# Begun blocks, sides, gate products, rotation and the first 1/rms of a two-sequence encoder layer, in another order

## The chip, the cores and the metric

One core of a Trainium2 chip runs the whole program in one launch. The metric is the device time of a launch in microseconds, of which the median over runs is taken. Two runs of one kernel that differ by less than about 0.2% are not told apart.

## The reference

Two sequences of 512 tokens by 1024 channels pass one layer. All data is float32.

```
def swiglu(x, w_gate, w_up, w_down):
    return (jax.nn.silu(x @ w_gate) * (x @ w_up)) @ w_down

def encoder_layer(x, ...):
    x = x + 0.5 * swiglu(rms_norm(x, ffn1_norm), ffn1_w_gate, ffn1_w_up, ffn1_w_down)
    h = rms_norm(x, mix_norm)
    proj = h @ w_in
    aq, ak, av, mq, mk, mv, gate_pre, o_pre, g_att, g_mlstm = jnp.split(proj, split_at, axis=-1)
    aq = apply_rope(rms_norm(aq, q_norm), cos, sin)
    ak = apply_rope(rms_norm(ak, k_norm), cos, sin)
    att = gqa_block_attention(aq, ak, av)
    mem = mlstm_bidirectional(mq, mk, mv, gate_pre, mlstm_gate_bias, o_pre, mlstm_head_norm)
    merged = jax.nn.sigmoid(g_att) * (att @ w_up_att) + jax.nn.sigmoid(g_mlstm) * (mem @ w_up_mlstm)
    x = x + merged @ w_out
    x = x + 0.5 * swiglu(rms_norm(x, ffn2_norm), ffn2_w_gate, ffn2_w_up, ffn2_w_down)
    return x
```

After the layer comes a last rms_norm. The FFN's hidden width is 2816 (22 blocks of 128), attention has 8 query heads and 2 key heads of 64 channels with a rotation by position, and the matrix memory (mlstm) has 4 heads of 128 channels in two directions, with running maxima that keep its exponentials in range.

## The kernel before

**Number format and products.** Each float32 operand is split into a high and a low part in TensorE's rounded format (ACT copies the high part, VectorE subtracts to get the low one), and each product is three matmuls: high by high, high by low, low by high. A 512 by 512 by 128 product is so 4 x 3 = 12 matmuls of 128x512 (`product`, L297).

**Stages.** FFN1 up, FFN1 down, the mix of sequence 0, the mix of sequence 1 with both output projections, FFN2 up, FFN2 down, output. Each FFN's product with its weights uses Strassen's scheme with seven products where eight would stand: the left factors are sums of gate and up weight halves, the right ones (`xc`) sums of halves of the two sequences, named B11, B21, B22, T4, T1, T2_, T3.

**FFN up.** 22 blocks of hidden columns, each with seven products into three banks of PSUM: X (mm) for B11 and B21, Y (pss) for T2_, T3, T4, and Z (pst) for T1 and B22. B11 and B21 need the first sequence alone, so some blocks (`AHEAD` of them) are *begun* early, while the second sequence is still normalised: their two results are written to memory (`kept`) and read back when the block is *resumed*, with five products then. `gu_rest` is the rest of a block: u2 is v1 plus T2_ (L326); v5 is a copy of T1 by ACT (L330); the add of T3 (L334), of v1 (L336), of B22 (L339), Silu (L341) and the add of T4 (L344) follow; and two gate products end it (L345, L346, on GpSimd). `ORDER` sets the order of blocks: a resumed and a whole block in turn, seven times, then the remaining eight whole ones. Two blocks make a pair.

**Sides.** After each block's gate products, `Sides` forms the right factors for the down stage and sends them to memory (`rbuf`): `out` copies the high part on ACT (L358), subtracts on VectorE (L359) and issues two DMAs on SyncE. `even` sends B11 of the first block of a pair, `odd` the other six.

**FFN down.** 28 steps of (product, chunk of pairs); its weights are loaded, summed and split on the way (`prep`), and the results are added to accumulators.

**Mix.** Keys and values with gates first, then queries with their norm and rotation (`q_rope`), eight attention heads with other projections filled in between (`fill`), the two up projections merged with tanh gates, and the four memory heads (`mem_head`). In `mem_head` a row of gate sums is loaded from `ebuf` to all partitions, GpSimd adds the triangular mask (L1022), VectorE takes two maxima (L1023, L1024), and some dozen tiny operations make the scales. The factor 1/rms of the first sequence (`mid_stats(0)`: transposes at L188, VectorE's steps at L166 to L177, a broadcast over TensorE at L198) is computed inside the first mix.

**What sets the order.** Instructions are issued by a scheduler that follows program order with priorities: `shifted(n)` moves what is issued inside it earlier (negative n) or later (positive n). Each engine and each queue then runs its list strictly in order, and waits at the first instruction whose operands are not there. `LATER` is 100 and `SOONER` -100. Buffers come from rings: a tile's next user waits for its last reader.

## Time and profile before

| what | value |
|---|---|
| runs of the kernel | 2181.13, 2179.64, 2176.89 us; median 2179.64 |
| the profiled execution | 2180.97 us, its span 2179.2 us |
| TensorE matmuls x9544 | 2096.6 us busy (96%) |
| VectorE x2881 | 1642.4 us (75%) |
| ACT x1699 | 954.3 us (44%) |
| GpSimd x220 | 284.3 us (13%) |
| mean TensorE clock granted | 0.988 |

The stages by the trace, in us from the span's start: FFN1 up 20 to 476, FFN1 down to 688, mix of sequence 0 to 1046, mix of sequence 1 and the output projections to 1496, FFN2 up to 1946, FFN2 down to 2153, output to 2179. In rows of the trace PE is TensorE's matmuls, PEld its weight loads, DVE VectorE, POOL GpSimd and SP SyncE, whose queue issues most DMAs. A timeline row has its start, its length in us, engine, line, operation, tiles and shapes, how many instructions it merges, and in brackets the idle time before it and what ended that. A group's row ends with busy time, mean ns of one, idle time before, and its releasers.

### The profile page before, as it was taken

To read this page: it belongs to the slowest core of one execution; us is meant where nothing else is said; L and a number is where in the kernel's file an instruction comes from. 1 tells how busy PE (TensorE), PEld (TensorE's weight loads), DVE (VectorE), ACT (ScalarE), POOL (GpSimd) and SP (SyncE) were. 2 spreads that over 40 slices of the span, in tenths; PEclk is the share of its full clock that TensorE was granted. 3 is DMA by queue.
4 is the path that set the end of the run, shared out by engine and by line. 5 is a ranking of instruction groups with operands and counts; after the bars stand their busy time and mean duration, and the time that the engine had idled before them with its cause. 6 is when DMAs were issued, how large, how long until landed. Compare 5 with 4: busy or idle time off the path is not lost.

```text
span 2179.2 us, 27321 instructions
## 1 busy us (share of the span) xinstructions
PE 2096.6 (96%) x9544; PEld 1707.3 (78%) x9544; DVE 1642.4 (75%) x2881; ACT 954.3 (44%) x1699; POOL 284.3 (13%) x220
## 2 busy tenths in 40 slices
PE   8999999999999999999999999999999999999997
PEld 6877777878888777878887887877777778878886
DVE  7888877776697797785649878766877777776695
ACT  7534443443224466463436664434434344443222
POOL 0111121111002100100121001011111111110002
PEclk9999999999999999999999999999999999999999
DMA  9565654479765122332351233357455544479752
GB/s 298 163 195 183 213 168 157 145 265 382 284 220 181 40 68 57 95 104 77 115 165 39 59 92 95 114 153 224 155 176 171 177 159 159 140 273 386 270 196 106
DMA packets 312473, 366.04 MB, mean 168 GB/s; under 512 B 18352, under 2 KB 208832, under 8 KB 311312
## 3 DMA queue, kind: packets, MB, share of 16 engines
q1 hardware_dynamic: 311744, 363.04, 50.8%
q0 software_dynamic: 592, 1.27, 0.3%
q8 instruction: 75, 1.23, 0.2%
q14 instruction: 62, 0.51, 0.1%
HBM read 255.15 MB, written 109.08 MB: 167 GB/s over the span
## 4 chain that ended last, share of the span: by engine, by line
PE 41%; DVE 7%; issue 4%; ACT 2%; POOL 1%; DMA 1%; DVEq 0%; SPq 0%; ACTq 0%; POOLq 0%
PE mm L707 14%; PE pss L297 5%; PE pst L297 4%; PE mm L541 4%; PE mm L297 2%; PE pss L541 2%; PE pst L541 2%; PE mm L691 2%; PE pso L541 1%; POOL t L346 1%; PE pso L1096 1%; PE pso L936 1%; PE pss L1047 1%; PE pss L910 1%; PE pst L929 1%
## 5 line engine op out<-in xcount | busy, mean ns | idle before, releaser
L707 PE MATMUL mm<-xh,w 128*128 128x512 f32 x896 | 293.4, 397 | 0.0
L297 PE MATMUL pst<-xc,w 128*128 128x512 f32 x1056 | 263.7, 399 | 22.3 <-ACT t L330 22.3
L297 PE MATMUL mm<-xc,w 128*128 128x512 f32 x1056 | 259.6, 393 | 7.0 <-ACT f L306 4.0
L297 PE MATMUL pss<-xc,w 128*128 128x512 f32 x1056 | 256.0, 391 | 3.9 <-DVE t L326 3.9
L297 PEld LDWEIGHTS pst<-xc,w 128*128 128x128 f32 x1056 | 202.6, 193 | 69.9 <-ACT t L330 27.4
L297 PEld LDWEIGHTS mm<-xc,w 128*128 128x128 f32 x1056 | 196.5, 188 | 54.5 <-ACT f L306 7.9
L297 PEld LDWEIGHTS pss<-xc,w 128*128 128x128 f32 x1056 | 197.0, 188 | 48.4 <-DVE t L326 7.7
L707 PEld LDWEIGHTS mm<-xh,w 128*128 128x128 f32 x896 | 167.4, 189 | 32.1
L541 PE MATMUL mm<-rt,w 128*128 128x512 f32 (+1 forms) x819 | 186.0, 383 | 0.2 <-DMA rt<-rbuf 0.2
L221 ACT ACTIVATE w<-wr 128x1024 fp32r<-128x1024 f32 (+1 forms) x112 | 114.7, 1029 | 153.5 <-issue 72.2
L707 PE MATMUL mm<-xl,w 128*128 128x512 f32 x448 | 176.9, 395 | 0.0
L541 PEld LDWEIGHTS mm<-rt,w 128*128 128x128 f32 x819 | 150.2, 188 | 30.4 <-DMA rt<-rbuf 0.6
L346 POOL TENSOR_TENSOR t<-t,t 128x512 f32<-128x512 f32 x44 | 73.1, 1661 | 715.1 <-ACT t L341 547.3
L256 DVE TENSOR_TENSOR w<-t,w 128x512 fp32r<-128x512 f32 x176 | 137.1, 793 | 38.3 <-ACT w L255 36.5
L255 ACT ACTIVATE w<-t 128x512 fp32r<-128x512 f32 x176 | 107.4, 627 | 128.9 <-DVE t L281 42.7
L222 DVE TENSOR_TENSOR w<-wr,w 128x1024 fp32r<-128x1024 f32 (+1 forms) x112 | 137.0, 1224 | 35.1 <-ACT w L221 34.6
L297 PE MATMUL pss<-xc,f 128*128 128x512 f32 x528 | 128.6, 392 | 0.6 <-DVE t L334 0.6
L297 PEld LDWEIGHTS pss<-xc,f 128*128 128x128 f32 x528 | 98.1, 188 | 24.5 <-DVE t L334 4.6
L609 ACT ACTIVATE w<-wr 128x512 fp32r<-128x512 f32 x72 | 44.4, 630 | 132.0 <-PE pso L541 63.6
L609 ACT ACTIVATE w<-t 128x512 fp32r<-128x512 f32 x82 | 51.8, 632 | 110.5 <-PE pst L541 62.3
L541 PE MATMUL pss<-rt,w 128*128 128x512 f32 x396 | 94.5, 390 | 3.4 <-DVE w L610 3.4
L707 PEld LDWEIGHTS mm<-xl,w 128*128 128x128 f32 x448 | 84.7, 189 | 16.2
(328 smaller groups left out, 3896.0 us busy)
## 6 DMA issues: line engine op xcount, KB each, us to landing
rt<-rbuf SPq DMA_DIRECT2D x154, 512.0 KB, 5.9
wr<-in_w_in_dram SPq DMA_DIRECT2D x72, 512.0 KB, 3.9
wr<-in_ffn_w_gate_dram SPq DMA_DIRECT2D x56, 512.0 KB, 4.7
rbuf<-tab SPq DMA_DIRECT2D x90, 256.0 KB, 2.7
wr<-in_ffn_w_up_dram SPq DMA_DIRECT2D x44, 512.0 KB, 4.1
rbuf<-t SPq DMA_DIRECT2D x88, 256.0 KB, 3.3
rbuf<-f SPq DMA_DIRECT2D x66, 256.0 KB, 3.0
rbuf<-R SPq DMA_DIRECT2D x64, 256.0 KB, 2.7
```

Of the source, the lines that this page charges most:

```text
L221: pin(nc.scalar.activation(hi, raw, AF.Copy))
L222: pin(lo_eng.tensor_tensor(lo, raw, f(hi), op=ALU.subtract))
L255: pin(nc.scalar.activation(t[:, 0], src, AF.Copy))
L256: pin(V_.tensor_tensor(t[:, 1], src, f(t[:, 0]), op=ALU.subtract))
L297: nc.tensor.matmul(p, a[:, k, :], xt[:, b, k, :], start=(first and k == 0 and i == 0), stop=(k == HK_ - 1 and i == 2), skip_group_check=True)
L346: G_.tensor_tensor(u2, u2, v5, op=ALU.mult)
L541: nc.tensor.matmul(p, u[:, a, d * P:(d + 1) * P], r[:, b, ts], start=(first and q == 0 and k == 0), stop=(q == len(us) - 1 and k == 2), sk ...
L609: nc.scalar.activation(hi, src, AF.Copy)
L691: nc.tensor.matmul(p[b][:, :N], a[:, k, bs], w_[:, kl, :], start=(k == 0 and i == 0), stop=(k == KD - 1 and i == 2))
L707: nc.tensor.matmul(p, a[:, k, :], b, start=(k == 0 and i == 0), stop=(k == n - 1 and i == 2))
L910: nc.tensor.matmul(p, qT[:, h, b * P:(b + 1) * P], kv[:, hk * 2 + j, :], start=(j == 0), stop=(j == 1))
L929: nc.tensor.transpose(p[:, b * P:(b + 1) * P], Ps[b][:, kb * P:(kb + 1) * P], ident)
```

## The change

Seven things are edited.

- FFN up: nine blocks are begun instead of seven (`AHEAD`), and B11 of one is issued ahead of B21 of the one before (`begin`, `begun`). The order of blocks has seven pairs of a resumed and a whole block, six whole blocks, and the last two resumed blocks at the end (`LAST`).
- The two gate products of a block are made on VectorE instead of GpSimd: 88 operations of 128x512.
- Sides: T1's side goes out in `even`, with one more tile; in `odd` only the sends of B21, T3, T2_ and T4 are issued later, not B22's and the differences.
- The rotation's product with the cosines (ten operations) is made on VectorE instead of GpSimd.
- The memory's maxima move from `mem_head` into the attention's loop (`mem_max`, one of eight rows per attention head), and the scales are computed at once for all four heads (`mem_scales`). `mem_head` loads its rows and adds the mask again (`mem_rows`), so this is done twice per row.
- The first sequence's 1/rms is computed inside the last steps of FFN1's down stage.
- Splits of weights in `load_w` are issued 60 places sooner.

TensorE's list, in FFN2's up stage, one resumed block of the kernel before: pss, pst and mm are banks of PSUM (Y, Z and X), xc the right factors, w and f the left ones. The rows are T2_, T1, a third of the next block's B11, B22, another third, T3, the last third, and the beginning of T4.

```order
L297 MATMUL pss_13531<-xc_12775,w_13363 128x512 x12
L297 MATMUL pst_13532<-xc_12776,w_13363 128x512 x12
L297 MATMUL mm_13629<-xc_12139,w_13510 128x512 x4
L297 MATMUL pst_13532<-xc_12778,w_13364 128x512 x12
L297 MATMUL mm_13629<-xc_12139,w_13510 128x512 x4
L297 MATMUL pss_13531<-xc_12777,w_13364 128x512 x12
L297 MATMUL mm_13629<-xc_12139,w_13510 128x512 x4
L297 MATMUL pss_13531<-xc_12779,f_1756_12621 128x512 x2
```

The same block of the changed kernel, in a block of other numbers:

```order
L301 MATMUL pss_13551<-xc_12713,w_13387 128x512 x12
L301 MATMUL pst_13552<-xc_12714,w_13387 128x512 x12
L301 MATMUL mm_13653<-xc_12091,w_13530 128x512
L301 MATMUL pss_13551<-xc_12715,w_13388 128x512 x12
L301 MATMUL pst_13552<-xc_12716,w_13388 128x512 x12
L301 MATMUL pss_13551<-xc_12717,f_1752_12573 128x512 x2
L301 MATMUL pss_13551<-xc_12717,f_1753_12574 128x512
```

T3 (the third pss row of twelve and more) stood behind B22 (the second pst row) with B11 pieces on either side, and stands now ahead of it, with one B11 matmul between T1 and T3; the other eleven go behind T4.

VectorE's list at the same place, up to the row that makes u2 (t<-t,pss). L359 and L365 are the low parts of sides, L256, L260, L278 to L284 and L288 belong to the weights of later blocks. The kernel before, its last twelve rows up to u2 (L326):

```order
L359 TENSOR_TENSOR t_1761_12626<-t_1761_12626,R_12633 128x512
L284 TENSOR_TENSOR t_1754_12619<-wr_13377,t_1754_12619 128x512
L359 TENSOR_TENSOR tab_12635<-t_1762_12627,tab_12635 128x512
L374 TENSOR_TENSOR t_1763_12628<-t_1763_12628,t_1765_12630 128x512
L359 TENSOR_TENSOR t_1765_12630<-t_1765_12630,R_12634 128x512
L376 TENSOR_TENSOR t_1762_12627<-t_1762_12627,t_1763_12628 128x512
L278 TENSOR_TENSOR t_1753_12618<-wr_13529 128x512
L256 TENSOR_TENSOR w_13514<-t_1755_12620,w_13514 128x512
L256 TENSOR_TENSOR w_13514<-t_1754_12619,w_13514 128x512
L359 TENSOR_TENSOR t_1763_12628<-t_1763_12628,tab_12635 128x512
L280 TENSOR_TENSOR t_1754_12619<-wr_13527,wr_13529 128x512
L326 TENSOR_TENSOR t_1765_12630<-t_1760_12625,pss_13531 128x512
```

And the changed kernel, from the add of the former block's T4 (L350) past u2 (L332):

```order
L350 TENSOR_TENSOR t_1754_12575<-t_1754_12575,pss_13405 128x512
L629 TENSOR_TENSOR f_1753_12574<-wr_13303,f_1752_12573 128x512
L351 TENSOR_TENSOR t_1758_12579<-t_1758_12579,t_1754_12575 128x512
L365 TENSOR_TENSOR R_12585<-t_1759_12580,f_1763_12584 128x512
L260 TENSOR_TENSOR w_13533<-t_1750_12571,w_13533 128x512
L379 TENSOR_TENSOR t_1759_12580<-t_1759_12580,t_1761_12582 128x512
L288 TENSOR_TENSOR t_1750_12571<-wr_13401,t_1750_12571 128x512
L332 TENSOR_TENSOR t_1761_12582<-t_1756_12577,pss_13551 128x512
L365 TENSOR_TENSOR tab_12587<-t_1758_12579,R_12586 128x512
L365 TENSOR_TENSOR t_1757_12578<-t_1757_12578,tab_12587 128x512
L260 TENSOR_TENSOR w_13534<-t_1751_12572,w_13534 128x512
L260 TENSOR_TENSOR w_13534<-t_1750_12571,w_13534 128x512
```

The row of u2 stood fourteen rows behind T4's add (L344, three rows ahead of the first row shown) and stands seven behind it now; the gate product L351 is one of the six between, and a side's difference (L379) another. On ACT four side copies (L364) stand ahead of T1's copy (L336) now, and three (L358) stood there before.

VectorE's list in the first mix where the queries are rotated, of the changed kernel (st is the tile of the memory's scales, box the ebuf row):

```order
L765 TENSOR_TENSOR t_447_5767<-t_416_5657,rs_5696 128x512
L769 TENSOR_TENSOR t_448_5769<-t_447_5767,tab_4271 128x512
L774 TENSOR_TENSOR t_449_5770<-t_447_5767,tab_4271 128x256 x2
L935 TENSOR_REDUCE st_5975<-box_5341 128x4
L776 TENSOR_TENSOR t_448_5769<-t_448_5769,t_449_5770 128x512
L882 TENSOR_TENSOR f_479_5902<-mm_5876,R_5218 128x512
```

The first reduction of `mem_max` (L935) stands ahead of the rotation's last add (L776); no such row was there before. L769 is the rotation's product, which GpSimd made.

TensorE's list around the transposes of the first 1/rms (L188). Before, among the key and value products of the first mix (L691):

```order
L691 MATMUL mm_5311<-w_5340,xh_4935 128x272 x2
L691 MATMUL mm_5311<-w_5340,xl_4936 128x272
L691 MATMUL pso_5312<-w_5340,xh_4935 128x272 x2
L691 MATMUL pso_5312<-w_5340,xl_4936 128x272
L188 MATMUL pst_5397<-ident,R_4940 128x128 x4
L691 MATMUL mm_5309<-w_5370,xh_4935 128x272 x2
L691 MATMUL mm_5309<-w_5370,xl_4936 128x272
L691 MATMUL mm_5310<-w_5370,xh_4935 128x272 x2
L691 MATMUL mm_5310<-w_5370,xl_4936 128x272
```

and now, in the last step of the down stage (L560), ahead of the mix's first products (L710):

```order
L560 MATMUL mm_5240<-rt_3747,w_3753 128x512 x6
L560 MATMUL mm_5240<-rt_3747,w_3754 128x512 x2
L188 MATMUL pst_5185<-ident,R_4956 128x128
L560 MATMUL mm_5240<-rt_3747,w_3754 128x512
L188 MATMUL pst_5185<-ident,R_4956 128x128 x3
L560 MATMUL mm_5255<-rt_3747,w_3753 128x512 x6
L560 MATMUL mm_5255<-rt_3747,w_3754 128x512 x3
L560 MATMUL pso_5270<-rt_3747,w_3753 128x512 x6
L560 MATMUL pso_5270<-rt_3747,w_3754 128x512 x3
L710 MATMUL mm_5360<-w_5351,xh_4951 128x272 x2
```

The transposes moved from the middle of the mix's first products to the last step of FFN1's down stage.

The diff:

```
@@
         pin(lo_eng.tensor_tensor(lo, raw, f(hi), op=ALU.subtract))
         return hi, lo
+    WEIGHTS = 60
     def load_w(view, lo_eng):
-        return split_w(fetch_w(view), lo_eng)
+        raw = fetch_w(view)
+        with shifted(-WEIGHTS):
+            return split_w(raw, lo_eng)
@@
-    def gu_first(W, xc, rows, between=None):
+    def gu_first_a(W, xc, v1):
         X = MM()
         product(X, W[B11], xc[B11], True)
-        v1 = rows(0)
         with shifted(SOONER):
             nc.scalar.activation(v1, X, AF.Copy)
-        if between:
-            between()
+        return X
+    def gu_first_b(X, W, xc, g0):
         product(X, W[B21], xc[B21], False)
-        g0 = rows(1)
         with shifted(SOONER):
             nc.scalar.activation(g0, X, AF.Silu)
-        return v1, g0
     def gu_rest(W, xc, got, ring, mid):
@@
             v1, g0 = got
             second()
         else:
-            v1, g0 = gu_first(W, xc, lambda i: ring("vh"[i]), second)
+            v1, g0 = ring("v"), ring("h")
+            X = gu_first_a(W, xc, v1)
+            second()
+            gu_first_b(X, W, xc, g0)
         u2 = ring("h")
         with shifted(SOONER):
             V_.tensor_tensor(u2, v1, Y, op=ALU.add)
@@
         product(Y, W[T4], xc[T4], False)
         with shifted(SOONER):
             V_.tensor_tensor(v1, v1, Y, op=ALU.add)
-        G_.tensor_tensor(g0, g0, v1, op=ALU.mult)
-        G_.tensor_tensor(u2, u2, v5, op=ALU.mult)
+        V_.tensor_tensor(g0, g0, v1, op=ALU.mult)
+        V_.tensor_tensor(u2, u2, v5, op=ALU.mult)
         return g0, u2
     class Sides:
@@
         def even(self, b11, b12):
             self.out(B11, b11)
             V_.tensor_tensor(b11, b12, b11, op=ALU.subtract)
+            self.out(T1, b11)
             self.b = b11, b12
         def odd(self, b21, b22):
             t1, b12 = self.b
-            self.out(B21, b21)
             self.out(B22, b22)
             V_.tensor_tensor(b12, b22, b12, op=ALU.subtract)
-            self.out(T3, b12, True)
             V_.tensor_tensor(b22, b22, t1, op=ALU.subtract)
-            self.out(T1, t1, True)
-            V_.tensor_tensor(b21, b21, b22, op=ALU.subtract)
-            self.out(T2_, b22, True)
-            self.out(T4, b21, True)
+            with shifted(LATER):
+                self.out(B21, b21)
+                self.out(T3, b12, True)
+                V_.tensor_tensor(b21, b21, b22, op=ALU.subtract)
+                self.out(T2_, b22, True)
+                self.out(T4, b21, True)
     LATER, SOONER = 100,-100
-    AHEAD = 7
-    ORDER = [j for p in zip(range(AHEAD), range(AHEAD, NF)) for j in p] + list(range(2 * AHEAD, NF))
+    AHEAD = 9
+    LAST = 2
+    ORDER = [j for p in zip(range(AHEAD - LAST), range(AHEAD, NF)) for j in p]
+    ORDER += list(range(2 * AHEAD - LAST, NF)) + list(range(AHEAD - LAST, AHEAD))
     class Up:
@@
         def begin(self, j, W):
             self.kept[j] = kept[j]
-            for t, d in zip(gu_first(W, self.xc, lambda _: self.ring("k")), kept[j]):
-                nc.sync.dma_start(d, t)
+            t = self.ring("k")
+            X = gu_first_a(W, self.xc, t)
+            nc.sync.dma_start(kept[j][0], t)
+            self.begun()
+            self.open = j, X, W
+        def begun(self):
+            if self.open:
+                j, X, W = self.open
+                t = self.ring("k")
+                gu_first_b(X, W, self.xc, t)
+                nc.sync.dma_start(kept[j][1], t)
+            self.open = None
         def left(self, j):
             return gu_left_a(self.fetch(j, (0,))[0])
@@
                     with shifted(LATER):
                         sides.even(*h)
                 elif i < NF - 1:
-                    with shifted(LATER):
-                        sides.odd(*h)
+                    sides.odd(*h)
@@
                              rq.unsqueeze(2).to_broadcast([P, 8, DA]), op=ALU.mult)
             o, m = T2(), T2()
             v4 = lambda x: x.rearrange("p (b h e) -> p b h e", b=nb, e=DA)
-            G_.tensor_tensor(v4(o), v4(n), cb, op=ALU.mult)
+            V_.tensor_tensor(v4(o), v4(n), cb, op=ALU.mult)
...
@@
             q_rope(b)
         go(mem_qk(0, 1), mem_qk(1, 0), mem_qk(1, 1))
+        st = spool.tile([P, 4, 2, 4, HM], F32, tag="st", bufs=1, name=nm("st"))
+        n1, bd, en, n2 = [st[:, i] for i in range(4)]
+        def mem_rows(h, d):
+            eb = T2(F32, "eb")
+            nc.sync.dma_start(eb, ebuf[d, h:h + 1, :].rearrange("a s -> (a s)").partition_broadcast(P))
+            em = T2(F32, "eb")
...
+            G_.tensor_tensor(em3, eb3, tabs[3][:, d].unsqueeze(1).to_broadcast([P, 4, P]), op=ALU.add)
+            return eb3, em3
+        def mem_max(h, d):
+            eb3, em3 = mem_rows(h, d)
+            V_.tensor_reduce(n1[:, d, :, h], em3, axis=AX.X, op=ALU.max)
+            V_.tensor_reduce(bd[:, d, :, h], eb3, axis=AX.X, op=ALU.max)
+        def mem_scales():
+            a_, x_, B_ = csv[:, 0], csv[:, 1], csv[:, 2]
+            V_.memset(en[:, :, 0], 0.0)
+            for i in range(3):
+                V_.tensor_tensor(en[:, :, i + 1], en[:, :, i], B_[:, :, i], op=ALU.add)
+                V_.tensor_tensor(en[:, :, i + 1], en[:, :, i + 1], bd[:, :, i], op=ALU.max)
...
+            nc.scalar.activation(en, en, AF.Exp, scale=-1.0)
         att = A([P, 4, 2, S], F32R, "att")
         afs = {}
@@
             nxt = scores(h + 1) if h + 1 < HA else None
             attend(h, Ps)
             Ps = nxt
+            mem_max(h // 2, h % 2)
             fill(1 if h < 4 else 2)
             if h == 2 and extra:
                 extra()
+        mem_scales()
         fill(99)
@@
         def mem_head(h):
             qk = qks[h]
...
+            ebs, ems = zip(*[mem_rows(h, d) for d in range(2)])
...
@@
         for t, kk, bank in ((x1l, k, PS), (x1u, k + HK_, PT)):
             p = turn(1, kk, [bank])
             nc.scalar.activation(t, p, AF.Copy, scale=g1[:, kk:kk + 1])
-        W.append(up.left(3 + k))
+        if k == 1:
+            up.begin(2, W[2])
+        for j in ((), (3, 4), (5, 6), (7, 8))[k]:
+            up.begin(j, up.left(j))
         put(xc[B22], k, x1u)
         right_sums(xc, k, x0l, x0u, x1l, x1u)
-        if k == 1:
-            up.begin(2, W[2])
-    for j in (3, 4, 5, 6):
-        up.begin(j, W[j])
+    up.begun()
     def late_x(j, ring):
@@
             emit_hl(xs[0][:, d, :], gm, d, *nhl[0])
         nc.sync.dma_start(xbuf[s][:, d, :], xs[s][:, d, :])
         accs[s] = sq_add(xs[s][:, d, :], accs[s], "R")
-    def mid_stats(s):
-        r[s] = stats(accs[s])
-        R[s] = bcast_cols(r[s])
+        if s == 0 and d == KD - 1:
+            mid_stats(0, 100, 140)
+    def mid_stats(s, a=0, b=0):
+        with shifted(a):
+            r[s] = stats(accs[s])
+        with shifted(b):
+            R[s] = bcast_cols(r[s])
@@
-    m0 = mix(0, *nhl[0], lambda: mid_stats(0), lambda: mid_stats(1), prep1)
+    m0 = mix(0, *nhl[0], None, lambda: mid_stats(1), prep1)
@@
             nc.sync.dma_start(t, src)
         normed(x1l, g2, R2[1], k)
         normed(x1u, g2, R2[1], k + HK_)
-        W.append(up.left(3 + k))
+        for j in ((3,), (4,), (5, 6), (7, 8))[k]:
+            up.begin(j, up.left(j))
         put(xc[B22], k, x1u)
         right_sums(xc, k, x0l, x0u, x1l, x1u)
-    for j in (3, 4, 5, 6):
-        up.begin(j, W[j])
+    up.begun()
```

More of the change, by code (lines that the diff above doesn't have):

```diff
@@ L390, in __init__ @@
             self.v = [w.rearrange("(k p) c -> p k c", p=P) for w in (wg, wu)]
-            self.kept = {}
+            self.kept, self.open = {}, None
             self.ring = Rings(s=["t2"] * 3, wd=["f2"] * 2, v=["t2"] * 3, h=["t2"] * 5, o=["f2"] * 2 + ["R"] * 2)
@@ L898, in mix @@
         go(mem_qk(0, 1), mem_qk(1, 0), mem_qk(1, 1))
+        st = spool.tile([P, 4, 2, 4, HM], F32, tag="st", bufs=1, name=nm("st"))
[4 more added lines that the diff above has]
+            em = T2(F32, "eb")
+            eb3 = eb.rearrange("p (b s) -> p b s", b=4)
+            em3 = em.rearrange("p (b s) -> p b s", b=4)
+            G_.tensor_tensor(em3, eb3, tabs[3][:, d].unsqueeze(1).to_broadcast([P, 4, P]), op=ALU.add)
[10 more added lines that the diff above has]
+                V_.tensor_tensor(en[:, :, i + 1], en[:, :, i + 1], bd[:, :, i], op=ALU.max)
+            V_.tensor_tensor(en, a_, en, op=ALU.add)
+            V_.tensor_tensor(n1, n1, x_, op=ALU.subtract)
+            V_.tensor_tensor(en, en, n1, op=ALU.max)
+            V_.scalar_tensor_tensor(bd, x_, -1.0, en, op0=ALU.mult, op1=ALU.subtract)
+            V_.tensor_tensor(n1, a_, en, op=ALU.subtract)
+            V_.tensor_tensor(n2[:, :, 2:4], n1[:, :, 2:4], B_[:, :, 1:3], op=ALU.add)
+            V_.tensor_tensor(n2[:, :, 1], n2[:, :, 3], B_[:, :, 1], op=ALU.add)
+            nc.scalar.activation(en, en, AF.Exp, scale=-1.0)
         att = A([P, 4, 2, S], F32R, "att")
```

36 lines of the change are left out of this document (4 added, 32 removed).

## The prediction

> **What bounds the kernel now.** The page comes first: engines, then the chain that ended last.
>
> ```profile
> PE 2096.6 (96%) x9544; PEld 1707.3 (78%) x9544; DVE 1642.4 (75%) x2881; ACT 954.3 (44%) x1699; POOL 284.3 (13%) x220
> PE mm L707 14%; PE pss L297 5%; PE pst L297 4%; PE mm L541 4%; PE mm L297 2%; PE pss L541 2%; PE pst L541 2%; PE mm L691 2%; PE pso L541 1%; POOL t L346 1%; PE pso L1096 1%; PE pso L936 1%; PE pss L1047 1%; PE pss L910 1%; PE pst L929 1%
> ```
>
> TensorE is the bound, and no matmul is removed, so all there is to gain is time in which it waits, or runs slowly after a wait. The odd entry is POOL t L346, a GpSimd multiply, in a chain of TensorE work. The waits view, TensorE's rows, shows who is waited for (total us, times, longest):
>
> ```profile
> PE pst L297 <- ACT t L330: 22.3, 12, 2.1
> ...
> PE mm L297 <- ACT f L306: 4.0, 5, 2.3
> PE pss L297 <- DVE t L326: 3.9, 6, 1.9
> PE pss L1047 <- DVE t L1063: 3.8, 2, 1.9
> PE pss L541 <- DVE w L610: 3.4, 2, 2.0
> ```
>
> One wait is worth more than the others together: B22 on pst for the copy at L330, twelve times, once in each resumed block that a whole pair surrounds. The timeline of one of them:
>
> ```profile
> 1576.04 1.66 POOL L345 TENSOR_TENSOR t<-t,t 128x512 f32<-128x512 f32 x1 [2.07 <-DVE t L344]
> ...
> 1577.73 0.63 ACT L358 ACTIVATE R<-t 128x512 fp32r<-128x512 f32 x1 [1.54 <-POOL t L345]
> ...
> 1579.98 0.68 DVE L374 TENSOR_TENSOR t<-t,t 128x512 f32<-128x512 f32 x1
> ...
> 1580.69 0.63 ACT L358 ACTIVATE f<-t 128x512 fp32r<-128x512 f32 x1 [2.33 <-DVE t L374]
> ...
> 1581.23 0.58 ACT L330 ACTIVATE t<-pst 128x512 f32<-128x512 f32 x1
> ...
> 1581.86 4.61 PE L297 MATMUL pst<-xc,w 128*128 128x512 f32 x12 [2.10 <-ACT t L330]
> ```
>
> T1's result is long there, but ACT runs in order: L330 stands behind side copies (L358), the last of which waits for VectorE's L374; that add, and another of the copies, wait in turn for the gate products on GpSimd. TensorE stands 2.10 us, and the twelve matmuls after it take 4.61 us.
>
> What a pair costs over its work, from a piece of the chain (start, us) and TensorE's timeline:
>
> ```profile
> 1599.33 2.72 PE pst L297 x12
> ```
>
> ```profile
> 1764.47 3.01 PE L297 MATMUL pst<-xc,w 128*128 128x512 f32 x12 [2.10 <-ACT t L330]
> ```
>
> ```profile
> 111.15 4.53 PE L297 MATMUL pst<-xc,w 128*128 128x512 f32 x12 [2.10 <-ACT t L330]
> ```
>
> ```profile
> 147.79 3.04 PE L297 MATMUL pst<-xc,w 128*128 128x512 f32 x12 [1.50 <-ACT t L330]
> ```
>
> A product is 12 matmuls in 2.72 us; a pair (7 products and 5) needs 12 x 2.72 = 32.64. From 1581.86 to 1764.47 lie five pairs: 182.61 / 5 = 36.52 each, 3.88 too long. Slow matmuls follow some waits of 2.10 (4.53 and 4.61 against about 3.0 for 12 in this view) and not the one of 1.50.
>
> **The change, part by part.**
>
> *Resumed blocks (T3 ahead of B22, gate products on VectorE, sides no longer late).* FFN2's six pairs lose 6 x 3.88 = 23.3 us. FFN1's six waits are the rest of the 22.3, that is 22.3 - 6 x 2.10 = 9.7, and the first has slow matmuls, 4.53 - 3.04 = 1.5: 11.2. Together 34.5 us can go. The order of the changed kernel puts T3's 12 matmuls and one more between T1 and B22 on TensorE, so L330's copy gets 13 x 0.227 = 2.95 us where it had 4 x 0.227 = 0.9; and the Sides rows in front of it no longer wait on GpSimd. What is late next is u2: T3 goes into the bank that u2's add has still to read. Between the read of the former block's T4 and that add VectorE now has six other rows, so the add ends eight operations after T4. Their pace:
>
> ```profile
> 1594.32 0.68 DVE L344 TENSOR_TENSOR t<-t,pss 128x512 f32<-128x512 f32 x1
> 1594.92 0.68 DVE L610 TENSOR_TENSOR f<-wr,f 128x512 fp32r<-128x512 f32 x1
> 1595.52 1.78 DVE L284 TENSOR_TENSOR t<-wr,t 128x512 f32<-128x512 f32 x1
> ```
>
> ```profile
> 1595.08 1.67 POOL L345 TENSOR_TENSOR t<-t,t 128x512 f32<-128x512 f32 x1 [1.23 <-DVE t L344]
> ```
>
> Operations start 0.60 apart, so the add ends at 8 x 0.60 + 0.08 = 4.9 us, against T2_ + T1 + one matmul = 25 x 0.227 = 5.67 us on TensorE: slack 0.8, less when VectorE starts late. The third row shows the other price of GpSimd: a VectorE operation that meets its multiply takes 1.78 instead of 0.68, 1.10 more. Moving 88 multiplies adds 88 x 0.60 = 53 us to VectorE and takes back up to 88 x 1.10 = 97, so its load does not rise. Load now, in a window with the stall in it:
>
> ```profile
> 1600.00:1650.00 50.00, 47.90 (x204) 38.93 (x203) 37.82 (x54) 20.77 (x35) 8.90 (x6) 0.97 0.46 150
> ```
>
> (TensorE, weight loads, VectorE, ACT, GpSimd, clock.) VectorE's 37.82 of 50 is 27.9 a pair; four multiplies more and the delays less: 27.9 + 2.4 - 4.4 = 26 to 30 of 32.64, room on the mean but not at every place. I leave 0.3 us of new waiting in each of the 18 resumed blocks, 5.4 (bounds 0 and 18 x 1.2). **Gain 34.5 - 5.4 = 29.1.**
>
> *The clock rule.* The windows' clock of 0.97 and the 4.61 belong to waits of 2.10 us. The Trainium skill (TensorE: Matmul & The Clock Gate, Why this matters for your kernels) asks only for no idle gaps over about 3 us. By that rule these waits are too short to slow anything, and the slow matmuls would have another cause and stay; the rows, slow after two of the waits of 2.10 and not after the one of 1.50, speak for the gap. It is a rival below.
>
> *Nine begun blocks.* The early part gets 18 products to cover the second half of the inputs instead of 14, 4 x 2.72 = 10.9 us more TensorE work ahead of the first resumed block, none of it added in all. Its worst wait:
>
> ```profile
> 1531.84 5.28 PE L297 MATMUL mm<-xc,w 128*128 128x512 f32 x22 [2.29 <-ACT f L306]
> ```
>
> B11 of the next block now comes between B11 and B21 of one, so the copies L306 have 2.72 us. Of the 4.0 us of L306 waits I take 3.5 (0 to 4.0). Eight more blocks' halves are written and read over both FFNs:
>
> ```profile
> t<-kept SPq DMA_DIRECT2D x28, 256.0 KB, 3.4
> ```
>
> 3.4 us to land, issued a block (13.6 us) ahead: nothing; if SP's queue were late by that cover, 10 us more would be needed. VectorE's relief should take half of the L326 waits, 2.0 of 3.9 (0 to 3.9).
>
> *Two resumed blocks last.* At down's start TensorE waits 3.4 us in two places for L610 splits of units whose buffers the last block frees late. With two resumed blocks last, begun early, VectorE has only the sums and sides of five products a block to finish. I take 2.4 (from -3, if the last two blocks leave VectorE behind, to 3.4).
>
> *First 1/rms in the down stage.* Now:
>
> ```profile
> 698.12 0.60 PE L188 MATMUL pst<-ident,R 128*128 128x128 f32 x4
> ...
> 703.01 0.65 PE L198 MATMUL pst<-ident,rs 128*128 128x128 f32 x4 [1.28 <-DVE rs L177]
> ...
> 705.11 1.19 PE L691 MATMUL mm<-w,xh 128*128 128x512 f32 x2 [1.44 <-DVE kv L770]
> ```
>
> The sums' transposes stand in the middle of the k, v products; the result is there 4.9 us later, after those products end, and the drain that scales by it starts only then. Moved some 12 us ahead the chain is off the path: 1.28 + 1.44 = 2.7 us gained (0 to 4 with slow matmuls behind). Weight splits that are made earlier are counted at nothing: VectorE does the same work, and no wait for them is in the rows above.
>
> *Memory maxima in the attention.* The mix's 16 reductions and its additions:
>
> ```profile
> L1024 DVE TENSOR_REDUCE st<-box 128x4 f32<-128x512 f32 x16 | 10.9, 680 | 1.7 <-DMA box<-ebuf 1.6
> L1023 DVE TENSOR_REDUCE st<-box 128x4 f32<-128x512 f32 x16 | 10.6, 671 | 3.8 <-POOL box L1022 3.8
> L1022 POOL TENSOR_TENSOR box<-box,tab 128x512 f32<-128x512 f32 x16 | 22.3, 1395 | 135.7 <-DMA box<-ebuf 135.7
> 757.00:860.00 103.00, 101.38 (x499) 80.35 (x498) 88.36 (x191) 64.59 (x130) 3.81 (x3) 1.00 0.21 57
> 1166.00:1260.00 94.00, 94.00 (x473) 75.98 (x472) 80.69 (x176) 58.24 (x119) 0.00 (x0) 1.00 0.21 57
> ```
>
> (The last two are windows over the two attentions.) Per mix (10.9 + 10.6) / 2 = 10.8 us of VectorE work goes into windows where it is busy 88.4 of 103 and 80.7 of 94: 99.1 and 91.4, just below full. The additions, and the loads of ebuf, are done twice, eight more a mix beside the same VectorE work. If each delays VectorE as above, 8 x 1.10 = 8.8: 107.9 of 103 and 100.2 of 94, over by 4.9 and 6.2. Between no loss and 11.1 I take the middle, **minus 5**. The first reduction stands among the rotation's rows and waits for an ebuf load: 1 us lost (0 to 3 per mix). What leaves the later stage shortens the L1047 wait: 2.5 of 3.8. The rotation's ten multiplies on VectorE, 10 x 0.60 against 10 x 1.10 of delay gone: nothing (-3 to 3).
>
> The Trainium skill (SBUF — State Buffer, Who interferes with whom) says that a GpSimd instruction reading SBUF and a VectorE instruction with two SBUF inputs take one shared port in turn, the later waiting for the whole of the other. The 1.78 us row agrees: it ends 0.55 after GpSimd does. The same section says reductions never contend, which leaves attention's other operations to pay; by it the loss would lie nearer 11 than 0.
>
> **Sum.** 29.1 + 3.5 + 2.0 + 2.4 + 2.7 - 5 - 1 + 2.5 = 36.2. The profiled execution took 2180.97 us (span 2179.2 and 1.8 around it): 2144.8. It lies 1.3 above the median 2179.64 of the runs, so I forecast 2143.
>
> **Rivals.**
>
> *VectorE is late at u2.* Then T3 waits in each resumed block. A wait of 1.0 us instead of 0.3 in 18 blocks, without slow matmuls, costs 18 x 0.7 = 12.6: 2156. For it: eight operations in a row with 0.8 us of slack. Against: VectorE is free a fifth of a pair. Chance 0.16.
>
> *Slower.* The same place, with VectorE 3 us late because the gate products and no-longer-late sides stand ahead of u2's add: each of 18 resumed blocks waits 2.1 us and runs 1.5 us slowly after it (4.53 - 3.04), 3.6 x 18 = 65 less the 5.4 already charged: 2143 + 59 = 2202. It decides from 18 x w - 5.4 = 36.2, a loss w of 2.3 us a block, that is a VectorE 2.9 us behind at T4's read. Against it: the mean load has 2.6 to 6 us a pair to spare. Chance 0.05.
>
> *Slow matmuls stay.* If the wait does not cause them, FFN2 keeps 6 x (3.88 - 2.10) = 10.7 and FFN1 1.5: 2155. Chance 0.05.
>
> *Attention fills VectorE.* The whole 11.1 instead of 5, and 3 per mix at the first reduction: 6 + 5 = 11 more, 2154. Chance 0.10.
>
> *The order does not help.* T1's copy still stands behind four side copies on ACT; if these come over 3 us late, the wait stays and only the small terms move: 2144.8 is raised by the 29.1 to 2174. Chance 0.03.
>
> **How the numbers follow.** The forecast case, 2127 to 2152 by the terms' bounds, has 0.61. A measurement tells about 0.2%, 4.4 us. Faster by more: 0.61 + 0.16 + 0.05 + 0.10 and the 0.03 but for a third, 0.94; I give 0.92, the same 0.03, slower 0.05. The range runs from 2124 to 2163: it takes in the cases at 2154 to 2156 with some spread and leaves out 2174, 2202 and the outer ends.
>
> **What would show it.** Right: the L330 row is gone from TensorE's waits; FFN2's resumed blocks come 32.7 to 33.5 us apart; the clock is 1.00 in windows from 1560 on; no multiply on GpSimd in the up stages; L198 has no wait and the first q matmul follows the k, v products within 1 us; VectorE is busy 95 us or more in the first attention. Wrong: a new wait of T3 on u2's add (L332 of the changed kernel) of over 1 us; pairs still 35 us or longer; TensorE below 95% in the attention windows, waiting for the score or softmax rows; a longer wait at down's start.

## The result and the profile after

The changed kernel takes **2120.79 us** (median of 4 runs, 2117.81 to 2123.26) against 2178.26 of the kernel before beside it: a ratio of 0.9734, 95% interval 0.9717 to 0.9751. It is 57.5 us faster, where 36.2 were forecast, and lies 3 us below the range. The direction and the place were right; the sum was too small. A second set of runs was made beside other kernels:

> The changed kernel itself once more, as the measure for the runs beside it on the same chip: 0.9734 of the kernel before, within 0.0017.

It gave 2119.15 us, 0.9729 (0.9716 to 0.9742).

The page of the changed kernel, engines and the chain by line:

```profile
PE 2073.5 (98%) x9544; PEld 1698.2 (80%) x9544; DVE 1637.2 (77%) x2895; ACT 955.5 (45%) x1693; POOL 150.1 (7%) x138
...
PE mm L726 17%; PE pss L301 17%; PE pst L301 11%; PE mm L560 8%; PE mm L301 7%; PE pst L560 4%; PE pss L560 4%; PE mm L710 4%; PE pso L560 3%; PE pso L710 1%; PE pso L989 1%; PE pso L1124 1%; PE pss L1075 1%; DMA wr<-in_ffn_w_gate_dram 1%; PE pst L982 1%
```

GpSimd is out of the chain, and VectorE is as busy as before (1642.4, now 1637.2 us). It has taken over 98 multiplies, but its count rises by 14 only, since the scales of the four memory heads are now made at once, in fewer tiny operations. The kernel with the maxima back in the heads, shown below, keeps those tiny operations; its VectorE has 98 instructions more than before (2979 against 2881) and is busy 1637.7 us. So what the moved multiplies add, the end of the delays beside GpSimd gives back, as forecast. TensorE's waits (total us, times, longest):

```profile
PE mm L1191 <- DMA raw<-in_x_prompt_dram: 4.9, 3, 2.6
PE pst L904 <- DVE t L629: 4.6, 4, 1.8
PE mm L710 <- DVE t L1056: 2.8, 2, 2.5
PE pss L963 <- ACT t L968: 2.7, 5, 0.8
PE pst L198 <- DVE rs L177: 2.4, 5, 0.7
PE mm L301 <- ACT f L309: 2.4, 3, 1.3
...
PE pss L301 <- DVE t L332: 0.4, 1, 0.4
```

The twelve waits for T1's copy (L330 before, L336 now) are gone, and so are those for L1063 and for the down stage's splits. The new wait that was feared, T3 for u2's add (L332), shows once among the matmuls, with 0.4 us; TensorE's weight loads wait for that add twelve times, 4 of them in FFN1's up stage and 8 in FFN2's. T3 of resumed blocks in the two up stages, from TensorE's timeline (start, us):

```profile
119.97 2.33 PE L301 MATMUL pss<-xc,w 128*128 128x512 f32 x9
...
285.65 1.55 PE L301 MATMUL pss<-xc,w 128*128 128x512 f32 x6
...
1554.04 2.14 PE L301 MATMUL pss<-xc,w 128*128 128x512 f32 x8
...
1718.71 2.58 PE L301 MATMUL pss<-xc,w 128*128 128x512 f32 x10
```

FFN2: (1718.71 - 1554.04) / 5 = 32.93 us a pair, 0.29 over the 32.64 of its matmuls; 0.3 a resumed block had been charged. FFN1: (285.65 - 119.97) / 5 = 33.14, which holds four transposes a pair besides. By the windows over the two up stages, first of the kernel before, then of the changed one (us, TensorE, weight loads, VectorE, ACT, GpSimd, clock):

```profile
24.00:476.00 452.00, 434.18 (x1907) 350.44 (x1906) 362.54 (x526) 204.70 (x345) 73.48 (x48) 1.00 0.58 188
1496.00:1946.00 450.00, 432.56 (x1857) 350.02 (x1856) 351.33 (x512) 191.67 (x318) 73.77 (x44) 0.98 0.53 177
```

```profile
24.00:456.00 432.00, 427.56 (x1907) 350.65 (x1906) 356.37 (x567) 206.59 (x345) 0.00 (x0) 1.00 0.64 211
1463.00:1887.00 424.00, 422.43 (x1857) 346.70 (x1856) 352.61 (x553) 191.10 (x317) 1.72 (x1) 1.00 0.61 200
```

With as many matmuls FFN1's up stage is 20 us shorter and FFN2's 26 (the windows are whole us); the clock of 0.98 is back at 1.00. That is 46 of the 60 us between the two profiled executions (spans 2179.2 and 2119.3). The other 14 us of the trace lie at the two starts of down (2.3 and 1.7), ahead of the first q product (3.6), and in the mixes (some 6.5).

### The profile page after: what moved, and what is told of

Same layout as the page of the kernel before. It is cut to its first block, busy times and chain, and to the rows that moved or that the text cites. A ratio compares the mean times of both kernels' runs of the same rounds, so it can differ in the third digit from the quotient of the medians.

```text
span 2119.3 us, 27353 instructions
## 1 busy us (share of the span) xinstructions
PE 2073.5 (98%) x9544; PEld 1698.2 (80%) x9544; DVE 1637.2 (77%) x2895; ACT 955.5 (45%) x1693; POOL 150.1 (7%) x138
## 4 chain that ended last, share of the span: by engine, by line
PE 84%; DVE 10%; ACT 2%; DMA 2%; issue 1%; SPq 0%; POOL 0%; DVEq 0%; ACTq 0%; POOLq 0%
PE mm L726 17%; PE pss L301 17%; PE pst L301 11%; PE mm L560 8%; PE mm L301 7%; PE pst L560 4%; PE pss L560 4%; PE mm L710 4%; PE pso L560 3%; PE pso L710 1%; PE pso L989 1%; PE pso L1124 1%; PE pss L1075 1%; DMA wr<-in_ffn_w_gate_dram 1%; PE pst L982 1%
## 5 line engine op out<-in xcount | busy, mean ns | idle before, releaser
L301 PE MATMUL mm<-xc,w 128*128 128x512 f32 x1056 | 252.9, 391 | 4.2 <-ACT f L309 2.4
L301 PE MATMUL pst<-xc,w 128*128 128x512 f32 x1056 | 253.7, 389 | 0.0
L301 PEld LDWEIGHTS pst<-xc,w 128*128 128x128 f32 x1056 | 198.2, 188 | 41.2
L560 PE MATMUL mm<-rt,w 128*128 128x512 f32 (+1 forms) x819 | 186.3, 383 | 0.0
L560 PEld LDWEIGHTS mm<-rt,w 128*128 128x128 f32 x819 | 150.2, 188 | 29.8
L222 DVE TENSOR_TENSOR w<-wr,w 128x1024 fp32r<-128x1024 f32 (+1 forms) x112 | 140.3, 1254 | 37.5 <-ACT w L221 36.2
L260 DVE TENSOR_TENSOR w<-t,w 128x512 fp32r<-128x512 f32 x176 | 118.6, 688 | 56.3 <-ACT w L259 53.8
L301 PEld LDWEIGHTS pss<-xc,f 128*128 128x128 f32 x528 | 99.1, 188 | 20.6
L560 PE MATMUL pst<-rt,w 128*128 128x512 f32 x396 | 93.7, 389 | 0.0
L560 PE MATMUL pss<-rt,w 128*128 128x512 f32 x396 | 93.6, 389 | 0.0
```

The source lines that it names most:

```text
L222: pin(lo_eng.tensor_tensor(lo, raw, f(hi), op=ALU.subtract))
L260: pin(V_.tensor_tensor(t[:, 1], src, f(t[:, 0]), op=ALU.subtract))
L301: nc.tensor.matmul(p, a[:, k, :], xt[:, b, k, :], start=(first and k == 0 and i == 0), stop=(k == HK_ - 1 and i == 2), skip_group_check=True)
L560: nc.tensor.matmul(p, u[:, a, d * P:(d + 1) * P], r[:, b, ts], start=(first and q == 0 and k == 0), stop=(q == len(us) - 1 and k == 2), sk ...
```

## The experiments

Times of runs on different chips are compared by their ratio to the kernel before that ran beside them; 0.001 is 2.2 us. The changed kernel stands at 0.9729 and 0.9734, its mean 0.9731.

### Gate products back on GpSimd

```
-        V_.tensor_tensor(g0, g0, v1, op=ALU.mult)
-        V_.tensor_tensor(u2, u2, v5, op=ALU.mult)
+        G_.tensor_tensor(g0, g0, v1, op=ALU.mult)
+        G_.tensor_tensor(u2, u2, v5, op=ALU.mult)
```

> The changed kernel with the two gate products of a block back on GpSimd (2120.8 us is the changed kernel's median, 2178.3 that of the kernel before). Theory A, the order of T3 and B22 does the work: T3 stays ahead of B22, so T1's copy keeps 2.7 us more, and the waits of TensorE on it stay gone; what comes back is VectorE's delay beside GpSimd, seen at the add of u2: 2122 to 2135 us, waits of T3 on u2's add under 1 us each. Theory B, GpSimd's slow gate products are the cause: the waits on T1's copy or on u2's add come back in at least twelve resumed blocks with 1.5 to 2.1 us each and slow matmuls behind: 2145 to 2160 us.

Measured: 2144.16 us, 0.9844 (0.9829 to 0.9858), 25 us slower than the changed kernel. The form of theory A, at nearly the price of theory B. T3 stays ahead of B22, and the waits are for u2's add. VectorE, GpSimd and TensorE at one of them:

```profile
1597.44 0.67 DVE L350 TENSOR_TENSOR t<-t,pss 128x512 f32<-128x512 f32 x1
...
1598.64 1.77 DVE L379 TENSOR_TENSOR t<-t,t 128x512 f32<-128x512 f32 x1
...
1600.94 0.68 DVE L332 TENSOR_TENSOR t<-t,pss 128x512 f32<-128x512 f32 x1
```

```profile
1598.19 1.67 POOL L351 TENSOR_TENSOR t<-t,t 128x512 f32<-128x512 f32 x1 [2.43 <-DVE t L350]
```

```profile
1598.28 2.88 PE L301 MATMUL pst<-xc,w 128*128 128x512 f32 x12
1601.67 1.65 PE L301 MATMUL pss<-xc,w 128*128 128x512 f32 x6 [0.51 <-DVE t L332]
```

A side's difference (L379) that meets GpSimd's product takes 1.77 us, and u2's add is late by it. The last two rows also show what a listed wait leaves out. Twelve matmuls from 1598.28 on make room for the next at 1598.28 + 2.72 = 1601.00; it starts at 1601.67, so 0.67 us are lost where 0.51 are listed, and the first matmuls after it are slower (6 in 1.65, not 1.52). Fifteen such waits are listed with 9.7 us. By the first matmuls of the stages FFN1's up stage is 11.4 us longer than in the changed kernel, FFN2's 9.4, and each start of down 2.

### Sides issued as before

```
     def even(self, b11, b12):
-        self.out(T1, b11)
...
                 elif i < NF - 1:
-                    sides.odd(*h)
+                    with shifted(LATER):
+                        sides.odd(*h)
```

> The changed kernel with the sides issued as before (all of odd later, T1's side in odd); B22 then stands ahead of T3 again on TensorE. Theory A (the order does the work): TensorE waits for T1's copy in the resumed blocks again, 0.5 to 2 us in each: 2130 to 2155 us. Theory B (GpSimd's gate products were the cause, and they stay on VectorE): the side copies come in time, no such wait over 0.5 us: 2120 to 2127 us.

(Of the three differences of `odd` the changed kernel issues two without delay; the one for T4 stands under `LATER` with its send.) Measured: 2132.6 us, 0.9794 (0.9779 to 0.9808), 14 us slower. The price is theory A's; the wait is not. B22 is ahead of T3 again, but TensorE waits for u2's add (L332, ten times, 6.0 us in all, longest 1.5) and not for T1's copy.

### The two edits on the kernel before, together and alone

The edits are the two above, turned round and made on the kernel before.

> The kernel before with the gate products on VectorE and the sides in the new order, nothing else. Theory A, these two carry the up stages and both starts of down: FFN1 up 18 us and FFN2 up 22 us or more shorter than before, 2178 - 44 = 2134 us, within 4. Theory B, as the prediction divided it, 29.1 here and 3.5 + 2.0 + 2.4 from the nine begun blocks and the last two: 2149 us.

> The kernel before with the gate products on VectorE, nothing else; T3 still stands behind B22. Theory A, the two edits overlap (each removes most of the stall alone): 2178 - 33 = 2145 us, about what undoing the sides left (13 us short of both). Theory B, they need each other, since B22 still waits for T1's copy behind the side copies: 2155 us or more.

> The kernel before with the sides in the new order, gate products still on GpSimd. Theory A, overlapping: 2155 us, 25 short of both. Theory B, the stall only moves to u2's add, which now stands close behind GpSimd's products: 2165 us or more, with waits for t L326 of over 1 us in most resumed blocks.

Measured: both 2130.6 us, 0.9786 (0.9773 to 0.98), 46 us faster than the kernel before; gate products alone 2147.68, 0.9859 (0.9828 to 0.9889), 31 us faster; sides alone 2150.21, 0.9874 (0.9848 to 0.9901), 28 us faster. The two edits overlap by some 12 us. The single edits are known to 6 or 7 us only, but the spans of the profiled executions say the same: 32 and 31 us shorter alone, 51 together. Each edit alone removes the wait for T1's copy and leaves waits for u2's add, in the waits views of gate products alone and of sides alone:

```profile
PE pss L297 <- DVE t L326: 7.7, 9, 1.5
```

```profile
PE pss L297 <- DVE t L326: 6.8, 12, 0.8
```

Together they leave no gap over 0.2 us in the resumed blocks, and both starts of down are as short (2.8 and 1.7 us less) as in the changed kernel, with seven begun blocks and none of them last.

### Seven begun blocks, none last

```
-    AHEAD = 9
+    AHEAD = 7
-    LAST = 2
+    LAST = 0
...
```

The two lists of blocks that are begun at each step are shortened to match.

> The changed kernel with seven begun blocks and none of them last, begun in turn as now. Predicted on record: 3.5 us for the early part and 2.4 for the two starts of down, 5.9 together; by the trace down starts gained 2.3 and 1.7 with their slow matmuls. Theory A, nine begun blocks and the order of the last two carry these: 5 to 9 us slower, the waits for w L629 at down's start and L309 in the early part back. Theory B, the sides and gate products freed VectorE, and these waits are gone without the nine blocks: within 2 us of the changed kernel.

Measured: 2122.55 us, 0.9744 (0.9731 to 0.9758); the changed kernel beside it 2119.15. That is 3 us, between the two theories (within 2, or 5 to 9) and nearer B; the intervals overlap, and the two up stages together differ by 0 to 1.5 us in the traces. The starts of down were cleared by the gate products and sides, not by nine blocks: they are as short here and in the kernel with these two edits alone. The early part is another matter. FFN2's waits for the copies of begun blocks (2.29 and 0.28 us before, for L306) are gone here, where B11 of one block still goes ahead of B21 of the one before; the kernel with the two edits alone, without that order, still has 1.33 and 0.28. No run takes that order out alone.

### The first 1/rms back in the mix

```
-        if s == 0 and d == KD - 1:
-            mid_stats(0, 100, 140)
...
-    m0 = mix(0, *nhl[0], None, lambda: mid_stats(1), prep1)
+    m0 = mix(0, *nhl[0], lambda: mid_stats(0), lambda: mid_stats(1), prep1)
```

> The changed kernel with the first sequence's 1/rms back inside the first mix. Theory A, it is worth the two waits it removes and the slow matmuls behind, 3.6 us by the distance from the first k, v product to the first q product (16.86 us before, 13.28 now): 3 to 4 us slower than the changed kernel. Theory B, the time is taken back in the attention, where VectorE is the bound: the q products start 3.6 us later, but the attention's last score does not, and the time is within 1 us of the changed kernel.

Measured: 2126.18 us, 0.9758 (0.9745 to 0.9772), 6 to 7 us slower. TensorE's timeline has the two waits again:

```profile
680.27 0.65 PE L198 MATMUL pst<-ident,rs 128*128 128x128 f32 x4 [1.29 <-DVE rs L177]
682.36 1.19 PE L710 MATMUL mm<-w,xh 128*128 128x512 f32 x2 [1.44 <-DVE kv L789]
```

The first q product comes 3.5 us later, the first score 5.0, and nothing is taken back in the attention: theory A in its form, but not in its price of 3 to 4 us; 1.5 us more are lost at the rotation.

### The rotation back on GpSimd, with the maxima in the attention and without

```
-            V_.tensor_tensor(v4(o), v4(n), cb, op=ALU.mult)
+            G_.tensor_tensor(v4(o), v4(n), cb, op=ALU.mult)
```

> The changed kernel with the rotation's ten products back on GpSimd. Theory A, the move is worth something, since from the first q matmul to the first score the changed kernel is 4.0 us shorter in the first mix: 2123 to 2129 us, the waits at the transposes of the rotated queries longer. Theory B, as predicted on record (VectorE's ten operations and GpSimd's delays cancel): 2119 to 2122 us, the 4.0 us stay.

> The changed kernel with the maxima back in the memory heads (that kernel took 2117.2 us) and the rotation's products back on GpSimd as well. Theory A, the rotation on VectorE is what the prediction missed in the mixes, and the maxima in the attention cover it up: without them the 4.4 and 4 us that each attention starts later are not taken back, 2117 + 8 = 2125 us, and from the first q product to FFN2's first product 787 us or more. Theory B, as predicted (nothing): 2116 to 2119 us and about 780 us.

Measured: with the maxima in the attention 2125.08 us, 0.9757 (0.9743 to 0.9772), 6 us slower; without them 2125.65, 0.9765 (0.9752 to 0.9778), against 0.9725 and 0.9719 of the same kernel with the rotation on VectorE: 9 us. Theory A both times. TensorE's timeline of the first of the two kernels:

```profile
714.19 1.06 PE L904 MATMUL pst<-ident,t 128*128 128x128 f32 x8 [2.39 <-DVE t L629]
...
720.95 1.06 PE L904 MATMUL pst<-ident,t 128*128 128x128 f32 x8 [1.57 <-DVE t L629]
...
726.96 1.07 PE L904 MATMUL pst<-ident,t 128*128 128x128 f32 x8 [1.07 <-DVE t L629]
...
732.40 1.07 PE L904 MATMUL pst<-ident,t 128*128 128x128 f32 x8 [0.93 <-DVE t L629]
```

Each block of rotated queries is turned on TensorE, and each turn waits for the rotation: four waits, 6.0 us. In the changed kernel the same four are 1.75 and 0.78 and two of nothing. The first score comes 4.5 us earlier there. Without the maxima the mixes keep what they start earlier: from the first q product to FFN2's first product they take 789.3 us with the rotation on GpSimd, and 779.5 and 780.1 (two traces) with it on VectorE. With the maxima a good part is lost again in the attention: the same stretch is 785.8 us against 784.2 and 783.4, some 2 us, and not the 6 of the runs. (The profiled execution is the fastest of its four, 2122.05 us; the intervals allow 2 to 10.)

### The memory's maxima

```
-            mem_max(h // 2, h % 2)
...
-        mem_scales()
...
         def mem_head(h):
...
+                V_.tensor_reduce(pm_[:, d], em3, axis=AX.X, op=ALU.max)
+                V_.tensor_reduce(bm[:, d], eb3, axis=AX.X, op=ALU.max)
...
```

> The changed kernel with the memory's maxima and scales back in each memory head, loaded once. Theory A, VectorE had room in the attention, so the move cost nothing there and removed the two waits of L1047 (1.85 and 1.93 us) with the slow matmuls after them: undoing it gives 2124 to 2130 us. Theory B, as predicted on record (5 us lost in the attentions and 1 at the rotation, 2.5 gained at L1047): undoing it gives about 2117 us, and shorter attention windows.

> The changed kernel with the maxima in the memory heads once more: 2117 us, 0.9725 of the kernel before (the changed kernel was 0.9729 to 0.9734), if they cost nothing within the noise; 0.971 or less if the 5 us that its profile is shorter hold.

Measured: 2117.21 us, 0.9725 (0.9709 to 0.9741), and again 2116.81, 0.9719 (0.9699 to 0.974): theory B. It is the lowest of the kernels that ran beside it, both times, 1 to 3 us below the changed one by the ratios. The intervals overlap, so the size stays open; another pair of kernels with the same difference, made below for the weight splits, is 4 us apart (0.9741 and 0.9723). The traces show where: VectorE in the first attention, windows of the changed kernel and of this one in its second set (after the length come TensorE, weight loads and then VectorE):

```profile
726.00:833.00 107.00, 102.93 (x508) 81.43 (x508) 100.29 (x207) 65.97 (x133) 10.93 (x9) 1.00 0.24 67
```

```profile
726.00:826.00 100.00, 99.04 (x493) 78.92 (x492) 87.64 (x191) 63.45 (x130) 2.73 (x2) 1.00 0.21 58
```

VectorE is busy 100.3 of 107 us with the maxima and 87.6 of 100 without, and TensorE loses 4.1 and 1.0. Beside the rotation the changed kernel has this, on VectorE and on GpSimd:

```profile
710.02 2.94 DVE L774 TENSOR_TENSOR t<-t,tab 128x256 f32<-128x256 f32 x2
712.89 0.67 DVE L935 TENSOR_REDUCE st<-box 128x4 f32<-128x512 f32 x1
```

```profile
709.81 2.87 POOL L929 TENSOR_TENSOR box<-box,tab 128x512 f32<-128x512 f32 x2 [27.94 <-DMA box<-ebuf]
```

The mask additions of mem_max hold up two rotation steps until they end, at 712.68; the steps take 2.94 us and elsewhere 0.75 together. What is given back is a wait of TensorE in the third memory head of each mix (L1065 here, 2.9 us in two waits), which the changed kernel does not have.

Two more kernels asked whether the place of the maxima matters; the second is made on the kernel with maxima in the heads:

```
-            mem_max(h // 2, h % 2)
...
         fill(99)
+        for h in range(HA):
+            mem_max(h // 2, h % 2)
+        mem_scales()
```

> The changed kernel with all eight mem_max of a mix written behind the attention's loop and its filled projections, so that they stand among the later heads. Theory A, the maxima cost where VectorE is full (first heads and rotation) and save at the first memory head: 2114 to 2117 us, with no wait of L1075. Theory B, any place in the attention costs the same: 2119 us.

```
+            if h == HA - 2:
+                first[1] = mem_scale(1)
...
```

> The maxima back in the memory heads but for the second head, whose maxima and scales are computed during the seventh attention head (its rows are loaded twice); the wait of L1065 of 1.55 and 1.41 us belongs to that head. Theory A, a quarter of the maxima fits into the attention: those two waits go and nothing else moves, 3 us less than the kernel with all maxima in the heads, 2114 us. Theory B, VectorE is full there and the attention gets longer by as much: 2117 us.

Measured: all maxima later in the attention 2121.74 us, 0.9747 (0.9733 to 0.976), no gain; only the second head's there 2118.53, 0.9732 (0.9712 to 0.9753), no better than none (0.9719 beside it).

The first of the two says that VectorE is full there: the waits in the memory heads stay gone, and what these save the attention spends. Its window of the first attention:

```profile
726.00:826.00 100.00, 95.93 (x470) 75.56 (x469) 93.05 (x190) 62.16 (x127) 12.62 (x9) 1.00 0.26 74
```

TensorE loses 4.1 us, against 1.0 with the maxima in the heads. The second kernel does not answer its question, because it moved the maxima of the wrong head. The two waits are still there, 1.98 and 1.15 us (L1082 of that kernel). They stand in the middle of the third head's products, which wait for VectorE's product with the weights (L1098), and VectorE's list has, by their order, the reductions and scales of the fourth head ahead of it:

```profile
917.61 1.28 DVE L983 TENSOR_REDUCE st<-box 128x4 f32<-128x512 f32 x2 [0.58 <-POOL box L973]
...
920.75 0.28 DVE L1098 SCALAR_TENSOR_TENSOR t<-pss,t 128x128 f32<-128x128 f32 x1
...
921.71 0.97 PE L1082 MATMUL pss<-qk 128*128 128x512 f32 x3 [1.98 <-DVE t L1098]
```

The second head's reductions had stood at 842 to 847 us (in the kernel with all maxima in the heads), far ahead of this place. Whether the fourth head's alone fit into the attention was not run.

### Weight splits not sooner

```
-    WEIGHTS = 60
+    WEIGHTS = 0
```

> The changed kernel with the weight splits no longer issued 60 places sooner. The prediction counted this edit at nothing; yet from the first k, v products of mix 0 to FFN2's first product the changed kernel with the maxima in the heads is 14.7 us shorter than the kernel before, of which the first 1/rms explains 3.6. Theory A, the earlier splits are what the prediction missed in the mixes: 5 to 10 us slower than the changed kernel, with waits for w L222 (split_w) back at the mix's products. Theory B, as predicted: within 2 us of the changed kernel.

> The changed kernel with the maxima back in the memory heads and no weight split issued sooner. Theory A, the earlier splits carry the rest of the mixes' gain and the full attention covered it up in the run with 0 places: 2120 to 2124 us. Theory B, they are worth nothing but the wait for w L222 of 2.6 us, which takes the place of the one for ml L629: 2116 to 2119 us.

Measured: 2121.3 us, 0.9741 (0.9727 to 0.9754), and with the maxima in the heads 2117.17, 0.9723 (0.971 to 0.9737). The first is 2 us above the changed kernel beside it (2119.15), inside the intervals, and the second is level with its partner: theory B, worth nothing that can be measured. The splits did remove a wait, which the kernel before has and both of these kernels have again:

```profile
PE mm L707 <- DVE w L222: 2.6, 1, 2.6
```

```profile
PE mm L726 <- DVE w L222: 2.6, 1, 2.6
```

But in the changed kernel TensorE waits 3.0 us at the same line for the operands mh and ml, waits that had been hidden behind this one.

## Why the prediction was right and wrong

**Right.** The wait for T1's copy went, as ordered by the lists. The charge for u2's add came out in FFN2, 0.3 us a block (measured 0.29); it had been chosen between 0 and 1.2, so the hit is in part luck. For FFN2's up stage 23.3 - 9 x 0.3 = 20.6 us were forecast, and 3.5 for the early parts of both stages, of whose waits 2.6 us lay in FFN2 and went: about 23, where 26 were measured. VectorE's load did not rise. The slow matmuls went with the waits, so the rival that they have another cause fell. By the rule of the Trainium skill (TensorE: Matmul & The Clock Gate, Why this matters for your kernels), which asks for no idle gaps over about 3 us, these waits should slow nothing; the windows here, 0.98 with waits of 2.10 us and 1.00 without, do not agree. The weight splits are worth nothing. The maxima were put at -5 - 1 + 2.5 = -3.5 us, of which the -5 was the middle between two bounds; the runs say -1 to -4 and their traces -3 to -5, with VectorE busy 100 us where 95 or more were named as the sign.

**Out of reach.** Even with every term at its best bound, and no loss in the attention, the prediction's sum is 34.5 + 4.0 + 3.9 + 3.4 + 4 + 3.8 + 3 = 56.6 us (the 3.8 is the whole wait of L1047). The 57.5 measured would have needed all of that at once, and the attention did lose time. So some terms had bounds that were too low.

**Wrong, first and largest: FFN1's share.** The step is "FFN1's six waits are the rest of the 22.3, that is 22.3 - 6 x 2.10 = 9.7, and the first has slow matmuls, 4.53 - 3.04 = 1.5: 11.2". With 2.0 of 3.9 for the waits behind it and 9 x 0.3 charged against it that is 10.5 us, where the up stage became 20 us shorter. FFN2 was priced by the distance from pair to pair, FFN1 by listed idle time, and that undercounts. TensorE's timeline of the kernel before has, four pairs behind the wait at 147.79 that the prediction shows:

```profile
288.60 2.56 PE L297 MATMUL pst<-xc,w 128*128 128x512 f32 x10 [1.54 <-ACT t L330]
```

(288.60 - 147.79) / 4 = 35.20 us a pair, and 33.14 now: 2.06 a pair beside waits listed with 1.5. Listed idle time runs from a matmul's modelled end (a single one is listed with 0.39 us) and not from where the next could have started (12 in 2.72 us, 0.227 apart), 0.16 of difference, and the first product afterwards is slower by some 0.15; small delays of T3 and T4 in the same blocks, too short to be listed, make up the rest. So the six pairs were worth about 14 (five at 2.06 and the first with its 2.10 and slow matmuls, 4), and the whole blocks behind them 6, their waits for VectorE and ACT all gone. Most of FFN1's nine charges of 0.3 had no ground: u2's add comes in time there in all but a few blocks.

**Wrong, second: the rotation.** The step is "The rotation's ten multiplies on VectorE, 10 x 0.60 against 10 x 1.10 of delay gone: nothing (-3 to 3)". It weighed VectorE's busy time. The rotation is a chain on which TensorE's turns wait one by one, and there GpSimd's operation stands in the chain itself, and delays the steps beside it. The sign stood in the waits view of the kernel before, in its second row, which the prediction's excerpt leaves out:

```profile
PE pst L885 <- DVE t L610: 6.0, 7, 2.0
```

L885 are the turns. With that row, and some twenty others left out, the wait for T1's copy is not worth more than all the others together, only more than those that were shown. With the rotation on VectorE and the maxima in the heads 1.8 and 1.5 us of these waits are left in two traces. The move is worth 9 us without the maxima, by runs and traces, and 6 with them by the runs (2 by the trace).

**Too small: the first 1/rms,** 2.7 by the two listed waits, 5 by the traces and 6 to 7 by the runs; the upper bound given with it was 4.

**Given to the wrong edit.** 3.5 + 2.4 for nine begun blocks and the last two: gate products and sides alone already cleared the starts of down, FFN2's early part probably by the order in which blocks are begun, and the block count is worth 0 to 3 us. The sum by single edits is 46.6 for gates and sides, 6 for the rotation, 6 for 1/rms, 0 to 3 for the blocks, 0 to 3 for the splits and -1 to -3 for the maxima, 56 to 64, against 58.

**Left out.** Of the weight splits the prediction says "no wait for them is in the rows above". That is true of the rows shown; the whole view has the wait of 2.6 us for one of them (L222). That the splits are worth nothing was right for another reason, the waits behind it. One small slip besides: VectorE's 37.82 of 50 us is 27.6 a pair of 36.52, not 27.9, and nothing hangs on it.

**Open.** Whether the maxima cost 1 us or 5, since no run resolves it, whether the rotation's move is worth 2 us or 6 with the maxima in the attention, what the fourth head's maxima alone would do there, and what decides whether slow matmuls follow a wait: they followed five of the seven waits of 2.10 us and not the other two.

## What to carry to other kernels

Price a stall by the distance between the same instructions of two rounds, not by the idle time that a waits view lists: here 2.06 us a pair stood beside listed waits of 1.5. Look for an engine that holds up another engine's in-order list before counting busy time; two edits that both unblock one list overlap, here by some 12 us of 58. Read the whole waits view before calling one wait the only one. When work is moved to fill an engine, look at what it is moved beside: at 88 of 103 us busy VectorE had no room for 11 more with GpSimd running next to it.

## What the runs showed of the hardware

Two VectorE operations of 0.75 us together took 2.94 while GpSimd added two masks, and ended 0.28 us after it (712.96 against 712.68). The Trainium skill (SBUF — State Buffer, Who interferes with whom) has this as a lock held for the whole instruction, and the rows agree; what had not been expected is its price on a chain, 9 us for ten multiplies where the maxima were not in the way. Nor had it been that a wait listed with 0.51 us costs 0.67 and slower matmuls behind it.
